# Moving the key, solution and delta-rule work of a woven decoder layer, and splitting its weight cuts over two steps

## The chip, the core and the metric

The kernel runs on one core of a Trainium2 chip. The core has a matrix engine (TensorE, PE in the profile), a vector engine (VectorE, DVE), a scalar engine (ScalarE, ACT), a general engine (GpSimd, POOL) and SyncE (SP), which here only issues transfers. Each engine works through its own list of instructions in order, and an instruction waits until the semaphores it names have been raised. Transfers (DMAs) are issued from the lists of SP, POOL and ACT. The metric is the device time in microseconds of one execution, as the median of several.

## The reference: what is computed

One inference step of a one-layer hybrid decoder over 512 new prompt tokens and 8 sampled tokens, all in float32, width 2048. Cut to what matters here:

```python
xn   = rmsnorm(h, norm_mix)
proj = xn @ w_in                      # columns: q | k | v | z | beta | decay | pool
qkv_c, new_conv = short_conv(conv_buf, qkv, conv_w)   # 4 taps, then silu
q = l2norm(q) * (DN_HEAD_DIM ** -0.5);  k = l2norm(k)
# gated delta rule, per head, chunks of the sequence:
a_mat = strict_lower(k k^T * beta * decay) + I
u, w  = triangular_solve(a_mat, v * beta), triangular_solve(a_mat, k * beta * exp(gc))
S     = S * exp(g_last) + k_dec^T @ (u - w @ S)       # from chunk to chunk
o     = (q * exp(g)) @ S + tril(q k^T * decay) @ v_new
dn_out   = rmsnorm(o, dn_norm) * silu(z)
pool_out = multiscale trailing-window mean minus token, times w_pool
h = h + concat(dn_out, pool_out) @ w_out
h = h + (silu(gate) * up) @ w_down    # gate, up = rmsnorm(h) @ w_gate_up
```

There are 8 heads of width 128. The matrix products must hold float32 accuracy. The kernel reaches it by cutting each operand into a high part `hi` and a low part `lo`, and adding three products: high by high, low by high and high by low.

## The kernel before, in words

**Stages.** On the profiled time axis: up to about 48 us the tokens are normalised and transposed; up to about 165 us the first column tiles of `w_in`, among them the eight tiles of keys, are multiplied in pairs, some of them by Strassen's scheme (`strassen`, with a callback `after(q, j)` that is called behind product j of pair q); from about 165 to 690 us runs the woven stage, which the change concerns; then follow the output projection, gate/up and down.

**The woven stage.** 28 column tiles of `w_in` and the pooling tiles are multiplied one after another, each with 96 matmuls (lines L184 to L186) in 16 steps of six. Between the steps a planner, class `Weave`, places side work: `weave.at(step, task)` starts a task, a Python generator, at a step, and each `yield n` in it says that its next piece comes n steps later. The planner runs when the program is built; what it fixes is the order of instructions on each engine. Tables at the top of the file give the starting steps: `KS` for the eight heads' `keys`, `ELIM` for the elimination, `D0` for the first delta rule. Nothing else than the order and the semaphores says when something runs.

**The tasks, in the order in which they come:**

- `keys(h)` loads the head's key columns, which the pair stage had stored to memory (`c_d`), and convolves them: one tap on ACT (L505), three on DVE (L508), silu on ACT (L510, with a load of its function table). The silu's result goes to PE: the Gram matrix of the keys (L1234) and transposes (L1237). ACT sums squares of the transposes (L1210), DVE forms the scales `sck`, the scaled Gram blocks `nn` (L1255) and scaled keys `kd` (L1257). `decay` (L1203) forms a decay mask `dm` from `gcb`, which is loaded from `gcr_d`. SP writes the diagonal 32x32 blocks of `nn` to `nd_d` and reads them back as `nb` (L1262, L1269), so that all heads' blocks lie side by side.
- `first_qv` loads and convolves q and v of head 0; `take_qv(h)` does it for the later heads, spread over the rule before.
- `eliminate` inverts all diagonal blocks at once, 31 pairs of DVE instructions (L1291, L1293), spread by an account of their work: a `yield` of one step for each 0.55 of `work`. SP writes the result to `ud_d` (L1303) and `load_u` reads it back as `utf`, for head 0 and then for head 1 (L1192, four transfers each).
- `delta(h)`, 26 steps for each head, solves with `utf` (matmuls from L1356 on, `uu` on DVE at L1377, matmul L1375) and runs the state from chunk to chunk: `R` (L1411), `W` on ACT (L1419), `S` (L1429) on DVE, with matmuls at L1408, L1416 and L1423 between them.
- sampled tokens' states (matmul L1511), and the pooling of the tiles, a run of DVE instructions from L1606 on.

**The weights' feed.** `feed` is called at every step. Every eight steps it loads half a tile of weights on SP (`feed_load`, 512 KB, L300) and cuts a half that was loaded 14 steps earlier (`feed_cut`, through `cut_raw`): `hi` on ACT (L308), then `lo` on DVE (L309), which reads `hi`. A product's tile goes from PE's accumulator to `ext` by DVE (L275), and POOL stores it to `c_d` (`stored`, L493).

Of the kernel before, what the change touches and what calls it, by code (L numbers as in the profile page):

```python
# [17 lines left out]
P = 128  # L18
# [8 lines left out]
FT = FF // P  # L27
EPS = 1e-6
POOLBUF = 15
KS, ELIM, D0 = (-5, 8, 21, 33, 44, 55, 66, 77), 104, 154  # L30
CHUNKS = ((0, 264), (264, 520))
HALF = NTOK // 2
FP = FT // 2
# [50 lines left out]
def decoder_kernel(ctx, tc, x_prompt, x_sample, state_delta, state_conv, state_pool, norm_mix, w_in,  # L84
# [410 lines left out]
    def convolution(x, t, place):  # L495

        ys = []

        def load():
            pool.memset(x[:, 0:3], 0.0)  # L500
            pool.dma_start(x[:, 3:3 + SEQ], c_d[t])

        def first():
            ys.append(place())
            act.activation(ys[0], x[:, 0:SEQ], AF.Copy, scale=cw(0, t))  # L505

        def tap(i):
            return lambda: dve.scalar_tensor_tensor(ys[0], x[:, i:i + SEQ], cw(i, t), ys[0], op0=ALU.mult, op1=ALU.add)  # L508

        return [load, first, tap(1), tap(2), tap(3), lambda: act.activation(x[:, 3:3 + SEQ], ys[0], AF.Silu)]  # L510

    def to_columns(o, t, ci, acc):
        c0, c1 = CHUNKS[ci]
# [288 lines left out]
    with tc.high_priority(offset=9 * AHEAD), tc.manual_schedule():  # L802
# [194 lines left out]
                b_raw[n] = load_raw(win_view(in_cols(b_order[n // 2]))[:, HG * (n % 2):HG * (n % 2) + HG, :])  # L997

        def feed_cut(n):
            if n in b_raw:  # L1000
                hi, lo = cut_raw(b_raw.pop(n))
                b_cut[n] = [(hi[:, k, :], lo[:, k, :]) for k in range(HG)]

        def feed(now):
            if (now + 10) % 8 == 0 and (now + 10) // 8 >= 2:
                feed_cut((now + 10) // 8)
            if now % 8 == 0:
                feed_load(now // 8 + 3)

# [4 lines left out]
        def after(q, j):  # L1014

            if (q, j) == (0, 1):
                gates(10)
            if q < len(pairs) - 1:
                return
            if j == 0:  # L1020
                pool.dma_start(b12, xs_d[0:8].rearrange("k p c -> p k c")[:, :, HALF:])
            if j == 2:
                nparts[1][0]()
            if j == 3:
                nparts[0][0]()
# [19 lines left out]
    with ExitStack() as p1:  # L1045
# [126 lines left out]
        def y_tile():  # L1172
            return d1tile("y", [P, SEQ], "y")

        def places(h):

            if h < 4:
                a, b = mixb[:, h, :], mixb[:, 4 + h, :]
            else:
                a, b = mixa[:, 4 + (h - 4) % 3, :], mixa[:, 7, :] if h % 2 == 0 else d1tile("vs", [P, SEQ], "nn")  # L1180
            return a[:, NB - 3:NTOK], b[:, 0:SEQ]

        def come_back(h):
            kd = kds[h] = d1tile("kd", [P, SEQ], "kd")
# [28 lines left out]


        def keys(h):
            x, nn = places(h)
            kT = x[:, 3:3 + SEQ]
            conv = convolution(x, 8 + h, y_tile)
            conv[0]()
            load_decay(h)  # L1220
            yield 5
            for f in conv[1:4]:
                f()
                yield 1
# [54 lines left out]
        def eliminate():  # L1279
# [7 lines left out]
            for t in range(31, 0, -1):  # L1287
                w = 32 - t
                tm = d1tile("tm", [P, 256], "tm")
                tv = tm[:, 0:t * w].rearrange("p (s j) -> p s j", j=w)  # L1290
                dve.tensor_tensor(tv, nb[:, 0:t, t:t + 1].broadcast_to([P, t, w]),  # L1291
                                  u[:, t:t + 1, t:32].broadcast_to([P, t, w]), op=ALU.mult)
                dve.tensor_tensor(u[:, 0:t, t:32], u[:, 0:t, t:32], tv, op=ALU.subtract)  # L1293
                work += 0.34 + t * w / 480
                if work > 0.55:
                    yield int(work / 0.55)
                    work %= 0.55
            ut = d1tile("nb", [P, 32, 32], "ut")
            dve.tensor_copy(ut, u.rearrange("p s j -> p j s"))
            utr = ut.rearrange("p s j -> p (s j)")  # L1300
# [15 lines left out]
        def take_qv(h):  # L1316
# [280 lines left out]
        def pooled(t, pe0, operands):  # L1597
# [74 lines left out]
        with tc.high_priority(offset=8 * AHEAD), tc.manual_schedule():  # L1672
            weave.feed = feed
            weave.add(states())
            for h in range(H):
                task = keys(h)
                if KS[h] < 0:
                    weave.at(KS[h] + next(task), task)
                else:
# [16 lines left out]
                    qkv_tile(t, w, 0 if i else 8)  # L1696
            pool_tiles((4, 5, 6), 20)
            w_last = weights_of(23)
            weave.feed = None
        p1.enter_context(tc.manual_schedule(engines={mybir.EngineType.PE}))  # L1700
        pool_tile(7, operands, w_last)
# [742 lines left out]
```

## Time and profile before

| What | Value |
|---|---|
| Median of 3 runs | 2235.96 us (2235.49 to 2237.29) |
| Profiled execution, its own time | 2237.41 us |
| Span of its profile | 2235.7 us |
| PE busy | 2153.5 us, 96% of the span |
| DVE, ACT, POOL busy | 79%, 43%, 21% |
| Mean granted clock of PE | 0.987 |

The profile shows one execution; times in it are microseconds from the start of its span. A row of the timeline gives start, duration, engine, line, operation, output <- inputs and shape, and in brackets how long the engine had been idle before it and what ended that. SPq is SP's list of transfers, where the duration is that of issuing. In a row that groups instructions stand the busy time and the mean of one in nanoseconds, then the idle time before them and its causes. A row of PE's waits gives the line, what it waited for, the total, the number of waits and the longest. "Granted clock" is the share of full clock that the chip let PE have.

### The profile page before, as it was taken

The page shows a single profiled execution, that of the slowest core. Times are in us where ns is not written, and L with a number is a line of the kernel's source. Part 1 is how long each engine was busy: PE and PEld are TensorE (multiplying, and loading weights), DVE is VectorE, ACT ScalarE, POOL GpSimd, SP SyncE. Part 2 cuts the span into 40 slices and gives each one's busy share as a digit, 9 for nine tenths or more (in the row PEclk, how much of TensorE's full clock was granted, in tenths as well). Part 3 has the DMA queues.
Part 4 walks back from the last instruction along what each step waited for, and adds up shares of the span by engine and source line. Part 5 has one row for each costly group of instructions (what it writes and reads, how often), then busy time and mean ns, then how long its engine had stood idle before and what let it go on. Part 6 is the DMA issues. An engine that isn't in the chain of part 4 may idle for free.

```text
span 2235.7 us, 43054 instructions
## 1 busy us (share of the span) xinstructions
PE 2153.5 (96%) x17737; PEld 2139.6 (96%) x17737; DVE 1771.9 (79%) x2612; ACT 970.4 (43%) x1476; POOL 480.2 (21%) x596
## 2 busy tenths in 40 slices
PE   7997888999999999999999999999999999999998
PEld 7997888998999999999999999999999999999998
DVE  7785674555649997989878888888888788887997
ACT  6344623444415555434434344343343534434554
POOL 2113321211101220233232332332102501103100
PEclk9999898999999999999999999999999999999999
DMA  8244543443243553455455454554444845537343
GB/s 266 76 133 135 148 145 103 131 120 88 73 137 117 163 154 96 138 154 151 141 166 148 141 156 145 165 147 137 138 133 133 281 128 163 158 108 229 98 114 115
DMA packets 449381, 316.99 MB, mean 142 GB/s; under 512 B 27808, under 2 KB 424505, under 8 KB 445841
## 3 DMA queue, kind: packets, MB, share of 16 engines
q1 hardware_dynamic: 424657, 223.14, 35.5%
q0 software_dynamic: 23360, 90.37, 12.4%
q8 instruction: 139, 2.28, 0.4%
q10 hardware_dynamic: 1168, 0.74, 0.1%
q14 instruction: 57, 0.47, 0.1%
HBM read 261.97 MB, written 52.87 MB: 141 GB/s over the span
## 4 chain that ended last, share of the span: by engine, by line
PE 67%; DVE 5%; ACT 2%; issue 1%; DMA 1%; POOL 0%; ACTq 0%; DVEq 0%; POOLq 0%
PE dn L316 20%; PE dn L315 20%; PE dn L317 20%; PE mm L184 1%; DVE lo L309 1%; PE mm L186 1%; PE mm L185 1%; DMA s<-in_state_delta_dram 1%; ACT hi L308 1%; DMA st<-a_d 1%; PE dn L1511 0%; DVE raw L337 0%; PE mm L315 0%; PE mm L316 0%; PE mm L317 0%
## 5 line engine op out<-in xcount | busy, mean ns | idle before, releaser
L309 DVE TENSOR_TENSOR lo<-raw,hi 128x1024 fp32r<-128x1024 f32 (+1 forms) x493 | 613.1, 1261 | 140.4 <-ACT hi L308 138.7
L308 ACT CAST hi<-raw 128x1024 fp32r<-128x1024 f32 (+1 forms) x493 | 501.2, 1029 | 464.0 <-DVE raw L337 218.1
L184 PE MATMUL mm<-xh,hi 128*128 128x264 f32 (+1 forms) x960 | 293.5, 306 | 5.2 <-DVE ext L275 3.8
L186 PE MATMUL mm<-xh,lo 128*128 128x264 f32 (+1 forms) x960 | 276.3, 288 | 2.8 <-DVE lo L151 2.1
L185 PE MATMUL mm<-xl,hi 128*128 128x264 f32 (+1 forms) x960 | 276.3, 288 | 1.3 <-DVE xl L620 1.1
L184 PEld LDWEIGHTS mm<-xh,hi 128*128 128x128 f32 x960 | 187.0, 195 | 6.0 <-DVE ext L275 4.0
L186 PEld LDWEIGHTS mm<-xh,lo 128*128 128x128 f32 x960 | 185.9, 194 | 3.7 <-DVE lo L151 2.7
L185 PEld LDWEIGHTS mm<-xl,hi 128*128 128x128 f32 x960 | 187.0, 195 | 1.9 <-DVE xl L620 1.9
L337 DVE TENSOR_TENSOR raw<-raw 128x1024 f32<-128x1024 f32 (+1 forms) x136 | 182.6, 1343 | 2.3
L316 PE MATMUL dn<-b21l,hi 128*128 128x260 f32 x620 | 175.7, 283 | 0.4 <-DVE b21l L2153 0.4
L317 PE MATMUL dn<-b21h,lo 128*128 128x260 f32 x620 | 175.4, 283 | 0.0
L315 PE MATMUL dn<-b21h,hi 128*128 128x260 f32 x620 | 174.9, 282 | 0.0
L317 PE MATMUL dn<-b11h,lo 128*128 128x260 f32 x612 | 173.2, 283 | 1.3 <-DVE lo L309 1.3
L316 PE MATMUL dn<-b11l,hi 128*128 128x260 f32 x612 | 173.3, 283 | 0.0
L315 PE MATMUL dn<-b11h,hi 128*128 128x260 f32 x612 | 172.7, 282 | 0.0
L315 PE MATMUL dn<-T1h,hi 128*128 128x260 f32 x556 | 158.1, 284 | 0.0
L316 PE MATMUL dn<-T1l,hi 128*128 128x260 f32 x556 | 157.7, 284 | 0.0
L1775 POOL TENSOR_TENSOR mixa<-mixa 128x520 f32<-128x520 f32 x22 | 51.4, 2334 | 494.5 <-DVE mixa L1769 494.5
L317 PE MATMUL dn<-T1h,lo 128*128 128x260 f32 x556 | 156.8, 282 | 0.0
L315 PE MATMUL dn<-B22h,hi 128*128 128x260 f32 x548 | 155.9, 284 | 0.0
L316 PE MATMUL dn<-B22l,hi 128*128 128x260 f32 x548 | 155.6, 284 | 0.0
L317 PE MATMUL dn<-B22h,lo 128*128 128x260 f32 x548 | 154.6, 282 | 0.4 <-DVE lo L309 0.4
(739 smaller groups left out, 6845.5 us busy)
## 6 DMA issues: line engine op xcount, KB each, us to landing
raw<-in_w_gate_up_dram SPq DMA_DIRECT2D x134, 512.0 KB
raw<-in_w_in_dram SPq DMA_DIRECT2D x75, 512.0 KB
a_d<-mixa POOLq DMA_DIRECT2D x22, 1040.0 KB, 5.5
raw<-in_w_down_dram SPq DMA_DIRECT2D x48, 448.0 KB
mixb<-in_w_gate_up_dram SPq DMA_DIRECT2D x41, 512.0 KB
raw<-in_w_out_dram SPq DMA_DIRECT2D x25, 512.0 KB
st<-a_d POOLq DMA_DIRECT2D x49, 260.0 KB, 6.5
raw<-in_w_down_dram SPq DMA_DIRECT2D x24, 512.0 KB
```

The lines of the kernel that those rows point to most:

```text
L184: te.matmul(acc[ci], wh, hi[k][:, c0:c1], start=(i == 0), stop=False)
L185: te.matmul(acc[ci], wh, lo[k][:, c0:c1], start=False, stop=False)
L186: te.matmul(acc[ci], wl, hi[k][:, c0:c1], start=False, stop=(i == len(w) - 1))
L308: act.copy(hi, raw)
L309: dve.tensor_tensor(lo, raw, hi.bitcast(F32), op=ALU.subtract)
L315: te.matmul(acc, wh[:, k, :], xf[:, k, :], start=start and k == 0, stop=False)
L316: te.matmul(acc, wh[:, k, :], xg[:, k, :], start=False, stop=False)
L317: te.matmul(acc, wl[:, k, :], xf[:, k, :], start=False, stop=stop and k == wh.shape[1] - 1)
L337: dve.tensor_tensor(r[name], r[a], r[b], op=op)
L1775: pool.tensor_tensor(q[:, 4:8:2, :], q[:, 1:4:2, :], q[:, 0:2, :], op=ALU.subtract)
```

## The change

It alters five things, all in the woven stage or just ahead of it.

1. **Keys.** `KS` becomes 4, 16, 28 ... 88, twelve steps apart, where it was -5, 8, 21, 33, 44, 55, 66, 77. A head's task no longer begins with its load and a pause of five steps, so that the Gram matmuls fall on steps 12, 24, 36, 48, 60, 72, 84, 96 (before: 9, 21, 34, 46, 57, 68, 79, 90). Heads 0 to 6 are loaded by SP during the last Strassen pair, head 7 at step 76. `place_k` says where a head's keys lie, `place_n` where its `nn` does.
2. **Loads of q and v** go from POOL's to SP's list too; 24 loads in all change list.
3. **Weights' feed.** `hi` is cut one step earlier than before (13 steps behind the load), `lo` where both stood before, a step later; a list `low_parts` carries it over.
4. **Elimination and delta rules.** `ELIM` goes from 104 to 111 and `D0` from 154 to 171; the elimination yields a step for each 0.48 of work.
5. **Pooling** writes its result `pw` into a part of `mixb` that is no longer used, instead of the buffer `y`.

```diff
-KS, ELIM, D0 = (-5, 8, 21, 33, 44, 55, 66, 77), 104, 154
+KS, ELIM, D0 = (4, 16, 28, 40, 52, 64, 76, 88), 111, 171
...
-        def load():
+        def load(eng=pool):
             pool.memset(x[:, 0:3], 0.0)
-            pool.dma_start(x[:, 3:3 + SEQ], c_d[t])
+            eng.dma_start(x[:, 3:3 + SEQ], c_d[t])
...
         def feed_cut(n):
-            if n in b_raw:
-                hi, lo = cut_raw(b_raw.pop(n))
-                b_cut[n] = [(hi[:, k, :], lo[:, k, :]) for k in range(HG)]
+
+            hi, lo = [wpl.tile([P, HG * P], F32R, tag=x, name=x) for x in ("hi", "lo")]
+            raw = b_raw.pop(n)
+            b_cut[n] = [tuple(x[:, P * k:P * k + P] for x in (hi, lo)) for k in range(HG)]
+            act.copy(hi, raw)
+            return lambda: dve.tensor_tensor(lo, raw, hi.bitcast(F32), op=ALU.subtract)
+
+        low_parts = []
 
         def feed(now):
-            if (now + 10) % 8 == 0 and (now + 10) // 8 >= 2:
-                feed_cut((now + 10) // 8)
+            if low_parts:
+                low_parts.pop()()
+            n = (now + 11) // 8
+            if (now + 11) % 8 == 0 and n in b_raw:
+                low_parts.append(feed_cut(n))
             if now % 8 == 0:
                 feed_load(now // 8 + 3)
...
+            if (q, j) == (2, 1):
+                for h in range(2, 7):
+                    convolution(place_k(h), 8 + h, None)[0](sp)
+            if (q, j) == (2, 4):
+                for h in range(2):
+                    convolution(place_k(h), 8 + h, None)[0](sp)
...
-            conv[0]()
             load_decay(h)
-            yield 5
+            if h == 6:
+                convolution(place_k(7), 15, None)[0](sp)
...
-                if work > 0.55:
-                    yield int(work / 0.55)
-                    work %= 0.55
+                if work > 0.48:
+                    yield int(work / 0.48)
+                    work %= 0.48
...
-                v[0]()
+                v[0](sp)
...
-            return [q[0], load_v, lambda: None, lambda: None, *q[1:5], lambda: (q[5](), v[1]()), *[lambda i=i: v[i]() for i in range(2, 6)]]
+            return [lambda: q[0](sp), load_v, lambda: None, lambda: None, *q[1:5], lambda: (q[5](), v[1]()), *[lambda i=i: v[i]() for i in range(2, 6)]]
...
-            pw = d1tile("y", [P, NTOK], "pw")
+            pw = mixb[:, t % 2, :]
...
-                if KS[h] < 0:
-                    weave.at(KS[h] + next(task), task)
-                else:
-                    weave.at(KS[h], task)
+                weave.at(KS[h], task)
```

Lines below the edits move: L308 and L309 of the feed become L1008 and L1009, the lines of `keys`, `decay`, `load_u` and `delta` grow by 13 (L1234 is L1247, L1356 is L1369).

**The loads of the keys.** POOL's list before, from the last store of the pair stage to the stage's first steps (`nt` are rows of the incoming states):

```order
L493 DMA c_d<-ext 128x512
L1021 DMA mixb<-xs_d 128x8x260
L500 MEMSET mixb 128x3
L501 DMA mixb<-c_d 128x512
L1088 DMA nt<-in_state_conv_dram 128x4x128
L1083 DMA nt<-in_state_conv_dram 64x128
L1088 DMA nt<-in_state_pool_dram 128x4x128
L1088 DMA nt<-in_state_pool_dram 128x3x128
L1083 DMA nt<-in_state_pool_dram 64x128
L500 MEMSET mixb 128x3
L501 DMA mixb<-c_d 128x512
L1147 MEMSET utf_2066 128x1024
```

and SP's list after the change, over the same stretch:

```order
L300 DMA raw<-in_w_in_dram 128x8x128 x3
L501 DMA mixb<-c_d 128x512 x2
L501 DMA mixa<-c_d 128x512 x3
L145 DMA raw<-in_w_in_dram 128x8x128 x2
L501 DMA mixb<-c_d 128x512 x2
L300 DMA raw<-in_w_in_dram 128x8x128 x2
L1209 DMA gcb<-gcr_d 128x512
```

Head 1's load stood on POOL behind the five transfers of states; now seven heads' loads stand on SP around the last weights of the stage before (L145).

**The solution's way to head 0.** SP's list before, behind the elimination:

```order
L1303 DMA ud_d<-u 28x4x1024
L1303 DMA ud_d<-ut 28x4x1024
L300 DMA raw<-in_w_in_dram 128x8x128
L1196 DMA gcb<-gcr_d 128x512
L1192 DMA utf_2066<-ud_d 32x8x32 x4
L1192 DMA utf_2068<-ud_d 32x8x32 x4
L300 DMA raw<-in_w_in_dram 128x8x128 x3
```

and after the change:

```order
L1316 DMA ud_d<-u 28x4x1024
L1316 DMA ud_d<-ut 28x4x1024
L300 DMA raw<-in_w_in_dram 128x8x128
L1205 DMA utf_2080<-ud_d 32x8x32 x4
L1209 DMA gcb<-gcr_d 128x512
L1205 DMA utf_2082<-ud_d 32x8x32 x4
L300 DMA raw<-in_w_in_dram 128x8x128
L501 DMA qT<-c_d 128x512
```

The decay vector `gcb` of head 0 came ahead of head 0's `utf`; now it stands between head 0's and head 1's. Head 1's q (`qT`) is new in this list.

**The cuts in a delta rule.** ACT's list before, at the start of head 1's rule:

```order
L1350 ACT_TABLE_LOAD
L1350 ACTIVATE gcb<-gcb 128x512
L1358 COPY xt__4182<-dn 128x384
L1359 ACTIVATE dm<-dm 128x512
L1210 ACTIVATE junk,ss<-dn 128x128 x4
L1210 ACTIVATE junk,so<-dn 128x128 x4
L308 CAST hi<-raw 128x1024
L505 ACTIVATE y<-qT,prm 128x512
```

and after the change:

```order
L1008 CAST hi<-raw 128x1024
L1363 ACT_TABLE_LOAD
L1363 ACTIVATE gcb<-gcb 128x512
L1371 COPY xt__4307<-dn 128x384
L1372 ACTIVATE dm<-dm 128x512
L1223 ACTIVATE junk,ss<-dn 128x128 x4
L1223 ACTIVATE junk,so<-dn 128x128 x4
L505 ACTIVATE y<-qT,prm 128x512
```

The cast `hi` moved from behind the eight sums of squares to ahead of the rule's first work on ACT. DVE's `lo` still stands just ahead of the rule's first `uu` there.

More of the change, by code (lines that the diff above doesn't have):

```diff
@@ L510, in convolution, with place_k @@
         return [load, first, tap(1), tap(2), tap(3), lambda: act.activation(x[:, 3:3 + SEQ], ys[0], AF.Silu)]
+    def place_k(h):
+        return (mixb[:, h, :] if h < 4 else mixa[:, 4 + (h - 4) % 3, :])[:, NB - 3:NTOK]
     def to_columns(o, t, ci, acc):
@@ L1173, in y_tile, with place_n @@
             return d1tile("y", [P, SEQ], "y")
-        def places(h):
-            if h < 4:
-                a, b = mixb[:, h, :], mixb[:, 4 + h, :]
-            else:
-                a, b = mixa[:, 4 + (h - 4) % 3, :], mixa[:, 7, :] if h % 2 == 0 else d1tile("vs", [P, SEQ], "nn")
-            return a[:, NB - 3:NTOK], b[:, 0:SEQ]
+        def place_n(h):
+            return (mixb[:, 4 + h, :] if h < 4 else d1tile("vs", [P, SEQ], "nn") if h % 2 else mixa[:, 7, :])[:, 0:SEQ]
         def come_back(h):
@@ L1215, in keys @@
         def keys(h):
-            x, nn = places(h)
+            x, nn = place_k(h), place_n(h)
             kT = x[:, 3:3 + SEQ]
             conv = convolution(x, 8 + h, y_tile)
-            conv[0]()
             load_decay(h)
-            yield 5
+            if h == 6:
+                convolution(place_k(7), 15, None)[0](sp)
             for f in conv[1:4]:
@@ L1676, in decoder_kernel @@
                 task = keys(h)
-                if KS[h] < 0:
-                    weave.at(KS[h] + next(task), task)
-                else:
-                    weave.at(KS[h], task)
+                weave.at(KS[h], task)
             weave.at(ELIM - 12, first_qv())
@@ L1698, in decoder_kernel @@
             w_last = weights_of(23)
+            assert not low_parts
             weave.feed = None
```

## The prediction

> **What bounds the kernel now.** I read the page first: which engine is full.
>
> ```profile
> PE 2153.5 (96%) x17737; PEld 2139.6 (96%) x17737; DVE 1771.9 (79%) x2612; ACT 970.4 (43%) x1476; POOL 480.2 (21%) x596
> ```
>
> TensorE (PE) is busy 96% of the span, so the kernel is bound by its matmuls, and only what delays PE can be won. Next I cut the span into stretches; after the stretch come its length, then busy us and instructions of PE, PE's weight loads, DVE, ACT and POOL, then the granted clock.
>
> ```profile
> 165.00:290.00 125.00, 100.44 (x768) 98.14 (x768) 76.38 (x194) 65.29 (x130) 45.20 (x103) 0.92 0.52 148
> 290.00:345.00 55.00, 39.73 (x296) 39.09 (x295) 35.49 (x84) 12.29 (x19) 5.99 (x12) 0.83 0.46 126
> 345.00:605.00 260.00, 241.23 (x1999) 237.35 (x1998) 150.38 (x343) 108.48 (x259) 39.94 (x80) 0.96 0.36 103
> 860.00:2000.00 1140.00, 1138.39 (x9451) 1137.69 (x9450) 976.33 (x1157) 477.33 (x621) 288.34 (x257) 1.00 0.51 149
> ```
>
> From 860 on there is nothing to win. The loss sits in the woven stage: PE idles 24.6 us during the keys (165 to 290), 15.3 during the elimination (290 to 345) and 18.8 during the delta rules (345 to 605), 58.6 in all. A weave step is six matmuls; at 1138.39/9451 = 0.12 us each that is 0.72 us. Then the waits of PE (total, times, longest):
>
> ```profile
> PE dn L1234 <- ACT mixb L510: 16.8, 3, 9.3
> PE dn L1356 <- DMA utf<-ud_d: 10.8, 1, 10.8
> PE dn L1375 <- DVE uu L1377: 7.3, 4, 3.0
> PE dn L1234 <- ACT mixa L510: 4.6, 3, 3.0
> PE mm L184 <- DVE ext L275: 3.8, 1, 3.8
> PE dn L1408 <- DVE S L1429: 3.1, 3, 1.3
> ```
>
> The keys' Gram matmul (L1234) waits 21.4 us for the silu, the first delta rule (L1356) 10.8 for the solution, the later rules mostly for DVE. Stalls also cost clock:
>
> ```profile
> 195.00:200.00 5.00, 5.00 (x25) 5.00 (x25) 2.48 (x4) 4.61 (x12) 1.49 (x7) 0.52 0.21 52
> 380.00:385.00 5.00, 4.71 (x31) 4.71 (x32) 2.83 (x12) 0.00 (x0) 2.65 (x4) 0.66 0.14 42
> ```
>
> After a long stall PE works at about half clock (25 matmuls in 5 us where 41 would fit). Over the three stretches the missing clock is 0.08 x 125 + 0.17 x 55 + 0.04 x 260 = 29.8 us; what falls into the idle time itself costs nothing, and I put the paid part at 7, 5 and 8, 20 us. So about 78 us are at stake.
>
> The second row follows a stall of only 1.9 us (shown below). The Trainium skill (TensorE: Matmul & The Clock Gate, "What's actually happening") has the clock halve after an idle window of about 3.4 us. By that rule the delta rules' short stalls would cost no clock; the row says they do, so the trace disagrees, and I keep the 8 us.
>
> **Keys.** POOL's, ACT's and PE's timelines at the two worst heads:
>
> ```profile
> 177.42 0.59 POOL L501 DMA_DIRECT2D mixb<-c_d  x1
> 184.87 0.72 ACT L505 ACTIVATE y<-mixb,prm 128x512 f32<-128x512 f32 x1 [5.05 <-DMA mixb<-c_d]
> 194.61 2.08 PE L1234 MATMUL dn<-mixb 128*128 128x128 f32 x8 [6.53 <-ACT mixb L510]
> 221.88 0.72 ACT L505 ACTIVATE y<-mixb,prm 128x512 f32<-128x512 f32 x1 [6.52 <-DMA mixb<-c_d]
> 228.86 1.01 PE L1234 MATMUL dn<-mixb 128*128 128x128 f32 x3 [9.30 <-ACT mixb L510]
> ```
>
> Heads 1 and 3 start their convolution 5.05 and 6.52 us late. For head 1 POOL issued the load at 177.42, 7.5 us before the tap, behind five other transfers. The change issues these loads before the stage, which takes 6.53 to 1.5 and 9.30 to 2.8. What remains is a loop: a head's convolution is queued behind the sums of squares that need the previous head's PE products. Its parts:
>
> ```profile
> L1210 ACT ACTIVATE junk<-dn 128x128 f32<-128x128 f32 x35 | 9.7, 276 | 3.2 <-PE dn L1237 2.1
> L1210 ACT ACTIVATION_READ_ACCUMULATOR junk<-dn 128x1 f32 x35 | 6.8, 194 | 0.0
> L505 ACT ACTIVATE y<-mixb,prm 128x512 f32<-128x512 f32 x4 | 2.9, 724 | 13.4 <-DMA mixb<-c_d 11.6 <-DVE mixa L536 1.7
> L510 ACT ACT_TABLE_LOAD x8 | 10.3, 1283 | 31.9 <-DVE y L508 31.9
> L510 ACT ACTIVATE mixb<-y 128x512 f32<-128x512 f32 x4 | 2.5, 630 | 1.3 <-issue 1.3
> L508 DVE SCALAR_TENSOR_TENSOR y<-mixb,prm,y 128x512 f32<-128x512 f32 x12 | 9.3, 772 | 6.4 <-ACT y L505 6.4
> L1255 DVE SCALAR_TENSOR_TENSOR mixb<-dn,sck,dm 128x128 f32<-128x128 f32 x16 | 4.8, 340 | 0.0
> L1257 DVE TENSOR_TENSOR kd<-dn,sck 128x512 f32<-128x512 f32 x8 | 5.4, 677 | 0.0
> L309 DVE TENSOR_TENSOR lo<-raw,hi 128x1024 fp32r<-128x1024 f32 x19 | 23.2, 1219 | 15.5 <-ACT hi L308 15.5
> ```
>
> About 1.2 us of matmuls, 4 x (0.28 + 0.19) of squares, 0.72, three taps 2.3, four `nn` 1.4, `kd` 0.7, silu with its table load 1.9: some 10 us, 1.2 more where a `lo` falls in. PE needs 12 steps, 8.6 us, plus 1.4 for the eight small matmuls: 10.0. The two are level, so a wait stays wherever `lo` or an eviction joins. By heads: 1.5 and 2.8 as above; head 2 (the third mixb wait, 16.8 - 6.53 - 9.30 = 1.0) loses a step (0.7): 1.7; heads 4 to 7 gain a step each, which takes their three waits, 4.6 together, to 2.9. That is 8.9. For heads 4 to 7 the third tap now comes behind all of `nn` and `kd` (at most 2 x 0.34 + 0.68 = 1.36 more each, 5.4); against that `lo` no longer makes DVE wait for `hi` (15.5 us in this stretch). I take 10.5. Idle falls by 11, the paid clock from 7 to 4: **14 us saved**, bounds 6 (the longer tap order counts in full and the clock stays) and 22 (the loop never binds).
>
> **Elimination.** The 3.8 us of L184 is a tile whose accumulator waits for an eviction behind the elimination on DVE, which comes behind head 0's q and v taps:
>
> ```profile
> L505 ACT ACTIVATE y<-qT,prm 128x512 f32<-128x512 f32 x1 | 0.7, 726 | 5.0 <-DMA qT<-c_d 5.0
> ```
>
> So it starts 5 us late for want of one load. That load moves to SP, 12 steps ahead as before, where no POOL work stands in front; and the elimination is spread over 21.9/0.48 = 45.6 steps instead of 21.9/0.55 = 39.8 (its work by the code's own sum), so evictions get more gaps: 3.8 to about 0.5, with 1.7 of clock: **5 us saved**, bounds 0 and 6.5.
>
> **The solution's way to head 0.** SP's queue, with what DVE and PE waited for:
>
> ```profile
> 323.92 0.68 SPq L1303 DMA_DIRECT2D ud_d<-u  x1
> 327.49 2.57 SPq L300 DMA_DIRECT2D raw<-in_w_in_dram  x1
> 330.12 2.56 SPq L1196 DMA_DIRECT2D gcb<-gcr_d  x1
> 332.79 7.66 SPq L1192 DMA_DIRECT2D utf<-ud_d  x8
> 340.15 1.14 DVE L1203 SCALAR_TENSOR_TENSOR dm<-gcb,gcs,mneg 128x128 f32<-128x128 f32 x4 [13.69 <-DMA gcb<-gcr_d]
> 340.88 0.93 PE L1356 MATMUL dn<-utf,mixb 128*128 128x96 f32 x3 [10.75 <-DMA utf<-ud_d]
> ```
>
> From the first write to PE's start are 17.0 us. The rule now starts 171 - 156.6 = 14.4 steps after the elimination's end by plan, instead of 154 - 143.8 = 10.2: 4.2 steps, 3.0 us more cover. `gcb` (2.56 us of issuing) goes behind head 0's four `utf` loads: 10.75 - 3.0 - 2.6 = 5.1. But then `gcb` lands last, and `dm` (1.14), ACT's exponentials and the copy of PE's product queue behind it; at worst all 2.6 come back. I take 6, with the paid clock from 3 to 2: **5.5 us saved**, bounds 1 and 9.
>
> **Delta rules.** One stall in full, on DVE and PE:
>
> ```profile
> L309 DVE TENSOR_TENSOR lo<-raw,hi 128x1024 fp32r<-128x1024 f32 x27 | 33.0, 1223 | 24.1 <-ACT hi L308 24.0
> 378.55 1.22 DVE L309 TENSOR_TENSOR lo<-raw,hi 128x1024 fp32r<-128x1024 f32 x1 [4.29 <-ACT hi L308]
> 380.29 0.38 PE L1375 MATMUL dn<-uu,xt__4182 128*96 128x64 f32 x2 [1.90 <-DVE uu L1377]
> 585.93 0.69 DVE L1606 TENSOR_TENSOR pes<-pe 128x518 f32<-128x518 f32 x1
> 590.70 0.35 DVE L1429 SCALAR_TENSOR_TENSOR S<-S,egl,dn 128x128 f32<-128x128 f32 x1
> ```
>
> DVE had 4.29 us with nothing to do, since `lo` waits for `hi` and `hi` stood behind eight sums of squares on ACT; `uu`, and PE with it, came after. With `hi` a step earlier and, at head 1, ahead of the squares, and `lo` between the rules' own operations, most of the 7.3 and 3.1 goes: 10 of 18.8 us idle, with `lo` itself (1.22) hidden in the time DVE waits for PE. Two things speak against: ACT's copy `xt` now stands behind a `hi` (about 1 us, where PE is late anyway), and the rules run 17 steps later, so that three instead of two pooling bursts (585.93 to 590.70, 4.8 us of DVE) meet heads 6 and 7: I add 2.5, at most 4.8. Idle 18.8 to 11.3, clock 8 to 5: **10.5 us saved**, bounds 3 and 21.
>
> **Costed at nothing or little.** 24 loads go from POOL to SP, whose queue is idle between weight loads; the five ahead of the stage's first weights are for tiles stored long before. If those weights were held up, the stage would start up to 3 us late. Tasks behind the rules come 10 steps later; PE work is the same. I add 2 us, 0 to 5. Memory conflicts: none counted.
>
> **Sum.** 14 + 5 + 5.5 + 10.5 - 2 = 33. The profiled execution took 2237.4 us (span 2235.7), so 2204.4 in its terms; it lies 1.4 above the median of 2235.96, and I forecast **2203 us**. All bounds at once would give 5 to 58.5 saved; the terms are nearly independent, so the forecast's own range is 2192 to 2215.
>
> **Rivals.** *The keys' loop still binds and DVE's stalls only move*: 6 + 2 + 4 + 6 - 1 = 17 saved, **2219**. For it: loop and PE are level at 10 us; against it: 11.6 us of the first tap's wait hung on loads alone. *SP becomes the queue that holds up the weights*: a q load stands in SP's order ahead of a weight load; if each of the eight heads' loads waits for its store and holds the weights by more than 33/8 = 4.1 us, `hi` and then L184 stall, at half clock, and the time goes above 2236, I say **2245**. For it: `gcb` and weight each took 2.6 us to issue; against it: weights are issued 13 steps, 9.4 us, before `hi`, and ACT's casts waited for no weight in the rules:
>
> ```profile
> L308 ACT CAST hi<-raw 128x1024 fp32r<-128x1024 f32 x27 | 28.1, 1041 | 0.0
> ```
>
> The Trainium skill (DMA: Bandwidth & Descriptors, "Issuing engines are not separate DMA queues") says that loads from all issuing engines share the same 16 DMA engines, so that moving them brings only the issuing time; no row here measures that, and my terms rest on issuing earlier. *No change*: one late step (the solution, say) gives back what the others win, **2236**. *The skill's clock rule after all*: the 3 us of clock in the delta rules are not won, **2206**.
>
> **Chances.** Forecast 0.66, loop 0.20, SP 0.06, no change 0.05, clock rule 0.03. A measurement tells 0.2%, 4.5 us. Faster: 0.66 + 0.20 + 0.03, less 0.02 for a slip beyond the cases: 0.87; same 0.06; slower 0.07. To leave out no more than 2 in 10 the range takes in the loop's case: 2190 to 2224.
>
> **What would show it.** In the changed kernel: no wait of ACT's first tap for `c_d` and L1234's successor idle 8 to 13 us; the solution's wait 4 to 8 us, with `gcb` landing after `utf`; DVE's `lo` waiting for `hi` under 5 us where it was 39.6; clock at least 0.95 in the keys. I am wrong if waits on the silu stay near 20 us, if ACT's `hi` waits for weights, or if the rules idle 18 us again.

## The result, and the profile after

The changed kernel takes 2219.1 us (median of 6 executions, 2213.18 to 2224.86) where the kernel before takes 2235.72 (6 executions, 2231.83 to 2237.29): a ratio of 0.9927, 95% interval 0.9909 to 0.9945, 16.6 us saved. The forecast was 2203. The direction was right, the size was not: half of the expected gain is missing. The time lies outside the forecast's own range (2192 to 2215), and inside the wider one (2190 to 2224), which had been drawn to take in a rival. The profiled execution took 2216.79 us, 20.6 less than that of before.

The first row is of the page, the others are the same kind of stretches as before, cut at the new boundaries (keys to 275, elimination to 327, rules to 590, then the rest of the woven stage; columns as in the prediction):

```profile
PE 2148.4 (97%) x17737; PEld 2135.9 (96%) x17737; DVE 1773.2 (80%) x2612; ACT 970.2 (44%) x1476; POOL 469.5 (21%) x572
```

```profile
165.00:275.00 110.00, 95.66 (x728) 93.00 (x727) 72.91 (x188) 64.04 (x128) 37.59 (x80) 0.94 0.53 152
275.00:327.00 52.00, 50.58 (x422) 50.37 (x421) 39.09 (x90) 11.46 (x12) 9.37 (x21) 1.00 0.50 147
327.00:590.00 263.00, 243.33 (x2052) 240.68 (x2052) 161.20 (x369) 118.14 (x278) 34.24 (x68) 0.97 0.38 108
590.00:680.00 90.00, 79.76 (x646) 78.74 (x646) 51.72 (x111) 28.66 (x46) 1.60 (x6) 0.94 0.37 103
```

The keys' and the elimination's stretches have improved: PE idles 14.3 and 1.4 us where it idled 24.6 and 15.3. The rules idle 19.7 us as before (18.8), and behind them, where the kernel before lost 2.6 us in 95 (605 to 700), PE now idles 10.2 in 90. PE's waits say at whom:

```profile
PE dn L1421 <- DVE S L1442: 7.2, 3, 3.8
PE mm L1729 <- ACT xh L210: 6.7, 1, 6.7
PE dn L1247 <- ACT mixb L510: 5.8, 3, 3.2
PE dn L1247 <- ACT mixa L510: 5.5, 4, 2.4
...
PE dn L1478 <- DVE mixb L1472: 3.3, 2, 3.1
...
PE dn L1421 <- DVE S L1440: 3.1, 1, 3.1
PE dn L1524 <- DMA s<-in_state_delta_dram: 3.0, 2, 1.8
PE dn L1388 <- ACT xt__6454 L1371: 2.3, 1, 2.3
...
PE dn L1388 <- ACT xt__5726 L1371: 1.9, 1, 1.9
...
PE dn L1369 <- DMA utf<-ud_d: 1.5, 1, 1.5
```

The keys wait 5.8 + 5.5 = 11.3 us (21.4 before), the solution 1.5 (10.8), the eviction of the elimination not at all (3.8). The first two rows are where new waits have come: PE waited for S 3.1 and 0.4 us before (L1429, L1427) and now 7.2 and 3.1 (L1442, L1440), and the output projection (L1729) waits 6.7 us for a split on ACT that had made PE wait 0.2.

**By parts.** I summed PE's waits of over 0.3 us in the timelines of all kernels, by the part of the woven stage in which they end. "Rules" are those between the first rule's start and some nine steps behind the last one's end, "tail" what comes then up to the output projection's first products (710 us). "Idle in all" is what PE's busy time leaves of the stretch from 160 to 710; besides the parts it holds some 3 us at the stage's entry, the same in all, and the waits under 0.3 us. The clock that was paid is the missing clock times PE's busy time in stretches of 5 us, from 160 to 710.

| Kernel | keys | elimination | solution | rules | tail | idle in all | clock paid |
|---|---|---|---|---|---|---|---|
| before | 21.2 | 4.5 | 10.8 | 18.5 | 2.2 | 61.1 | 18.7 |
| changed | 11.4 | 0 | 1.5 | 19.1 | 11.4 | 46.9 | 14.0 |
| before, cuts split | 20.3 | 4.5 | 10.3 | 11.8 | 3.3 | 54.0 | 12.0 |
| changed, cuts not split | 13.5 | 2.1 | 2.0 | 19.4 | 9.6 | 50.1 | 18.5 |
| changed, D0 161 | 10.2 | 0 | 9.5 | 13.7 | 4.3 | 41.1 | 12.5 |
| changed, hi three steps ahead | 10.9 | 0 | 1.7 | 11.7 | 10.7 | 38.4 | 11.8 |

Changed against before: 14.2 us idle and 4.7 us clock, 18.9 of the 20.6 us between the two profiled executions. The question for the experiments is the columns of the rules and the tail. A row is one execution, and its clock is partly chance, as the last section shows.

**A stall in the rules.** ACT, DVE and PE at the largest one, in head 2:

```profile
400.13 1.28 ACT L510 ACT_TABLE_LOAD   x1
401.42 0.63 ACT L510 ACTIVATE qT<-y 128x512 f32<-128x512 f32 x1
402.13 0.72 ACT L505 ACTIVATE y<-vT,prm 128x512 f32<-128x512 f32 x1
402.76 0.41 ACT L1583 ACTIVATE mixa<-mixa 128x264 f32<-128x264 f32 x1
403.07 1.03 ACT L1008 CAST hi<-raw 128x1024 fp32r<-128x1024 f32 x1
404.13 1.23 DVE L1009 TENSOR_TENSOR lo<-raw,hi 128x1024 fp32r<-128x1024 f32 x1 [3.49 <-ACT hi L1008]
405.28 0.34 DVE L1442 SCALAR_TENSOR_TENSOR S<-S,egl,dn 128x128 f32<-128x128 f32 x1
405.67 0.58 PE L1421 MATMUL dn<-S,mixb 128*128 128x128 f32 x1 [3.76 <-DVE S L1442]
```

It is the mechanism of before at another place. There eight sums of squares stood ahead of `hi`; here the next head's silu, its table load, a tap and an activation of a product's tile (L1583) do, 2.9 us from 400.13 to `hi`. One step, 0.72 us, is not enough lead. The same at 532.50 in head 6 costs 2.7 us. A second kind is the pooling run:

```profile
518.84 0.70 DVE L1619 TENSOR_TENSOR pes<-pe 128x518 f32<-128x518 f32 x1
...
522.91 0.70 DVE L211 TENSOR_TENSOR dl<-mixb,dh 128x520 fp32r<-128x520 f32 x1 [0.69 <-ACT dh L210]
523.53 0.28 DVE L1440 COPY S<-dn 128x128 f32<-128x128 f32 x1
523.87 0.58 PE L1421 MATMUL dn<-S,mixb 128*128 128x128 f32 x1 [3.11 <-DVE S L1440]
```

4.8 us of DVE in one piece, and S behind it (head 6). Two more such runs end at the copy `xt` of head 7 (2.3 us) and at the gate of head 7 (L1478, 3.1 us).

**The tail.** DVE, ACT and PE at the end of the stage:

```profile
657.52 0.28 DVE L1554 SCALAR_TENSOR_TENSOR mixa<-sc_qts,prm,mixa 128x64 f32<-128x64 f32 x1
...
660.20 2.21 ACT L210 CAST xh<-mixa 128x520 fp32r<-128x520 f32 x4 [1.94 <-DVE mixa L219]
660.88 0.59 PE L1729 MATMUL mm<-xh,hi 128*128 128x260 f32 x1 [6.75 <-ACT xh L210]
```

L1554 is the last operation of the sampled tokens' chain. Their tasks begin only when the last rule has ended (at step 379 by plan instead of 369), so the chain ends, at 657.8, after PE has run out of tiles, at 654.1, and the output projection, which begins with `mixa`, waits.

### The profile page after: what moved, and what is told of

Same layout as the page of the kernel before. It is cut to its first block, busy times and chain, and to the rows that moved or that the text cites. A ratio compares the mean times of both kernels' runs of the same rounds, so it can differ in the third digit from the quotient of the medians.

```text
span 2215.1 us, 43081 instructions
## 1 busy us (share of the span) xinstructions
PE 2148.4 (97%) x17737; PEld 2135.9 (96%) x17737; DVE 1773.2 (80%) x2612; ACT 970.2 (44%) x1476; POOL 469.5 (21%) x572
## 3 DMA queue, kind: packets, MB, share of 16 engines
q0 software_dynamic: 21440, 84.07, 11.6%
## 4 chain that ended last, share of the span: by engine, by line
PE 67%; DVE 5%; DMA 2%; ACT 1%; issue 1%; POOL 0%; ACTq 0%; DVEq 0%; SPq 0%; POOLq 0%
PE dn L316 20%; PE dn L315 20%; PE dn L317 20%; PE mm L184 1%; DVE lo L309 1%; PE mm L185 1%; PE mm L186 1%; DMA st<-a_d 1%; DMA s<-in_state_delta_dram 0%; DVE raw L337 0%; PE dn L1524 0%; ACT hi L308 0%; PE mm L315 0%; PE mm L316 0%; PE mm L317 0%
## 5 line engine op out<-in xcount | busy, mean ns | idle before, releaser
L308 ACT CAST hi<-raw 128x1024 fp32r<-128x1024 f32 (+1 forms) x447 | 453.3, 1028 | 445.5 <-DVE raw L337 217.3
L309 DVE TENSOR_TENSOR lo<-raw,hi 128x1024 fp32r<-128x1024 f32 (+1 forms) x447 | 556.8, 1265 | 102.7 <-ACT hi L308 101.2
L184 PE MATMUL mm<-xh,hi 128*128 128x264 f32 (+1 forms) x960 | 291.8, 304 | 1.5 <-ACT hi L149 1.5
L184 PEld LDWEIGHTS mm<-xh,hi 128*128 128x128 f32 x960 | 185.9, 194 | 2.0 <-ACT hi L149 1.9
```

The lines of the kernel that those rows point to most:

```text
L184: te.matmul(acc[ci], wh, hi[k][:, c0:c1], start=(i == 0), stop=False)
L308: act.copy(hi, raw)
L309: dve.tensor_tensor(lo, raw, hi.bitcast(F32), op=ALU.subtract)
```

## The experiments

Theory, from the trace: the split of the cuts works, but the new start of the rules (D0 171) takes its gain back, by pooling runs that meet the rules and by the sampled states' late chain. Rivals: the split does nothing, since ACT is blocked ahead of `hi` anyway; it is the phase of the rules against the eight-step cuts, not their lateness; the queue from which the loads are issued matters. Each kernel is given with its median, the kernel before's median on the same chip, and the ratio.

### The split alone, and everything but the split

The changed kernel with both cuts at one step:

```diff
-            n = (now + 11) // 8
-            if (now + 11) % 8 == 0 and n in b_raw:
-                low_parts.append(feed_cut(n))
+            n = (now + 10) // 8
+            if (now + 10) % 8 == 0 and n in b_raw:
+                feed_cut(n)()
```

> The changed kernel with the weights' cuts as before: hi and lo at the same step, lo right behind. If the split over two steps is what shortened DVE's wait for hi (39.5 us in the stage before, 21.1 changed), the wait goes back above 35 us and the time rises by 5 to 12 us over the changed kernel's 2219, to 2224 to 2231. Rival: the order of the keys and the earlier loads did it and hi is held up by what stands before it on ACT, not by its step: within 4 us of 2219.

Measured: 2223.1 against 2236.48, 0.9942 (0.9927 to 0.9957): 13.4 us saved. DVE's wait for `hi` went back as expected (below), but the time rose by 4 us only, under the 5 to 12. And the kernel before with nothing but the split of the feed:

> The kernel before, with only the cuts split over two steps. If the split is worth what I put on the rules (10.5 us forecast), 2224 to 2230, with DVE's wait for hi falling from 39.5 us to 20 or less and the rules' waits on uu and S (10.4 us) to half. Rival: ACT is blocked ahead of hi as often, the waits only change place: 2233 to 2238.

Measured: 2222.13 against 2236.48, 0.9936 (0.9922 to 0.9951): 14.3 us saved, a little more than expected, with a wait of 22.9 us where I had put 20 or less. DVE's waits for `hi` in the woven stage, in the kernel before, before with the split, changed, and changed without the split:

```profile
DVE lo L309 <- ACT hi L308: 39.5, 21, 4.6
```

```profile
DVE lo L1004 <- ACT hi L1003: 22.9, 15, 3.5
```

```profile
DVE lo L1009 <- ACT hi L1008: 21.1, 11, 5.3
```

```profile
DVE lo L1009 <- ACT hi L1008: 43.7, 21, 5.7
```

The split halves the wait in both settings. In the kernel before that is worth 14.3 us: 6.7 us less idle in the rules (18.5 to 11.8) and 6.7 us less clock (18.7 to 12.0). In the changed kernel it is worth some 4 us, with intervals that overlap (0.9927 to 0.9957, 0.9909 to 0.9945); by the table it helps there the keys and the elimination (13.5 to 11.4, 2.1 to 0) and the clock (18.5 to 14.0), and leaves the rules where they were (19.4 to 19.1). The two halves of the change save 13.4 and 14.3 us alone and 16.6 together. So the rival that the split does nothing falls, and part of the missing gain is an interaction in the rules: what the split wins there at the old start, it does not win at the new one. The tail's cost is another part, and it stands without the split too (9.6 us).

### The rules' start

Ten steps earlier:

```diff
-KS, ELIM, D0 = (4, 16, 28, 40, 52, 64, 76, 88), 111, 171
+KS, ELIM, D0 = (4, 16, 28, 40, 52, 64, 76, 88), 111, 161
```

> The changed kernel with D0 161 in place of 171. If the rules' lateness cost the tail, the 6.7 us wait of the output projection and the 3.0 us of the sampled states' matmuls go (with some 2 us of clock, 11 us won), while the first rule's wait for the solution grows from 1.5 by ten steps, 7.2 us, to 8.7 (with 2 us of clock, 9 lost): 2213 to 2221. Rival: the tail's wait comes from the pooling result's place in mixb or from the weights and stays at 6 us: then 2225 to 2230.

Measured: 2207.66 against 2236.48, 0.9874 (0.9858 to 0.9891): 28.8 us saved, 12 more than the change and better than either expectation. PE's waits:

```profile
PE dn L1369 <- DMA utf<-ud_d: 9.5, 1, 9.5
PE dn L1421 <- DVE S L1442: 6.9, 3, 3.8
```

L1729 has gone from the list and L1524 fell from 3.0 to 1.1: the tail's cost is the rules' lateness (the sampled tokens' tasks begin at step 369 again, as in the kernel before). The solution's wait grew by 8.0 us for ten steps, as expected. What I had not expected is the rules' own part, 19.1 to 13.7. By the timelines the larger share is the cuts: S behind `lo` costs one wait of 2.4 us (at 436) instead of 3.8 and 2.7. The pooling runs still meet S twice, for 3.8 and 2.6 us (at 534 and 557), 6.4 us instead of 8.5. A start later by ten steps thus bought 8 us at the solution for 7 in the tail, 5.5 in the rules, and clock.

One step earlier, which puts the eight-step cuts on the same places of the rules as in the kernel before (154 and 170 leave the same remainder):

> The changed kernel with D0 170 in place of 171, so that the cuts, which come every eight steps, fall on the same places of the rules as with 154. If this phase is what cost the rules their gain, PE's idle time in the rules falls from 19.5 to 11 to 14 us and the time to 2208 to 2213. Rival: the lateness alone counts: the solution's wait grows by 0.7, the tail's falls by 0.7, and the time stays at 2217 to 2221.

Measured: 2215.01 against 2234.34, 0.9912 (0.9896 to 0.9929). Between the two expectations, but idle in the rules went only to 16.2, far from the 11.8 of the same phase at the old start: the phase alone does not explain it. The rules' longest waits are at other operations than at D0 171:

```profile
PE dn L1429 <- DVE R L1424: 6.5, 3, 3.6
...
PE dn L1388 <- DVE uu L1390: 4.7, 3, 3.1
```

With the elimination at 0.55 per step again, and D0 165:

> The changed kernel with the elimination spread at 0.55 of work per step as before (39.8 instead of 45.6 steps) and D0 165, so that the solution's way has the same cover and the rules and the tail come 6 steps earlier. If the tail's cost goes by the rules' start, the output projection's wait falls from 6.7 to about 2.5 and the time to 2209 to 2216. Rival: the faster elimination brings the accumulators' wait back (3.8 us before) and the total stays at 2217 to 2222.

Measured: 2212.55 against 2236.48, 0.9896 (0.9881 to 0.991). The tail's idle fell from 11.4 to 4.3 us; the accumulators' wait came back with 0.8 us only. The solution's wait, which I took to stay the same, was 5.1: DVE does not keep the pace of 0.55 per step, so the elimination did not end 5.8 steps earlier as its plan says. SP's first write behind it stands at 314.98 us, against 314.68 in the changed kernel.

### What stands ahead of `hi`

`hi` three steps ahead of `lo` instead of one, `lo` where it was:

```diff
-            if low_parts:
+            if low_parts and (now + 10) % 8 == 0:
                 low_parts.pop()()
-            n = (now + 11) // 8
-            if (now + 11) % 8 == 0 and n in b_raw:
+            n = (now + 13) // 8
+            if (now + 13) % 8 == 0 and n in b_raw:
```

> The changed kernel with hi cut three steps ahead of lo instead of one. If the remaining stalls of S behind lo come from hi standing behind a head's silu and its table load on ACT, DVE's wait for hi falls from 21.1 us to under 10, the waits on S at L1442 from 7.2 to under 2 and the time to 2209 to 2214. Rival: hi then stands ahead of xt and the squares elsewhere or its weights are not there yet, and waits on xt or for the weights take the place: 2217 to 2223.

Measured: 2205.33 against 2234.34, 0.9868 (0.9853 to 0.9883): 29.0 us saved. DVE's wait for `hi`:

```profile
DVE lo L1009 <- ACT hi L1008: 8.3, 4, 3.5
```

21.1 to 8.3; the waits on S at L1442 left PE's list (the 3.76 us above and 2.7 us in head 6) but for 0.75 us, the rules' idle fell to 11.7, and the time by more than I gave it. At the place of the stall shown above, ACT now runs the cast while it would have been idle, ahead of the copy `W` and the silu with its table load (399.75):

```profile
395.59 1.05 ACT L1008 CAST hi<-raw 128x1024 fp32r<-128x1024 f32 x1 [0.77 <-PE mm L185]
```

In the kernel before the same edit, on top of the split:

> The kernel before with the cuts split, hi three steps ahead of lo in place of one (2222 with one). If hi standing behind other work on ACT is what is left of DVE's wait for it (22.9 us), it falls under 10 us and the time to 2212 to 2219. Rival: with the old start of the rules the split had already won what there is: 2220 to 2224.

Measured: 2213.58 against 2235.65, 0.9901 (0.9886 to 0.9915), 22.1 us saved by the cuts alone. DVE's wait for `hi` is 3.0 us there and the rules' idle 7.5. At the same cuts, then, the rules idle 7.5 us with the old start and 11.7 with the new one; this 4 us is about what the new start costs in the rules when `lo` hardly waits. The three pooling collisions (3.1, 2.3 and 3.1) are the longest waits at the new start, and the only ones over 0.3 us left there behind 510 us, 8.5 us; at the old start the rules' waits behind 510 us come to 2.4 us (1.2, 0.5 and 0.7).

### The pooling runs

Tiles 4, 5 and 6 pooled three steps after the tile's end (with the tile's buffer taken when its first half is evicted):

```diff
-            for _ in pooled(t, pe0, operands):
-                if weave.now <= SPLIT:
-                    pass
+            late = pooled(t, pe0, operands)
+            if t in (4, 5, 6):
+                weave.at(weave.now + 3, late)
+            else:
+                next(late)
```

> The changed kernel with the pooling run of tiles 4, 5 and 6 three steps later than the end of the tile. If the pooling runs are what stands before S, the copy xt and the gate at heads 6 and 7 (3.1, 2.3 and 3.1 us), these three waits fall to 3 us in all and the time to 2211 to 2215. Rival: the run then stands before another operation of the same rules, and the time stays at 2216 to 2222.

Measured: 2220.65 against 2234.34, 0.994 (0.9925 to 0.9955), no gain over the change. The waits moved instead of going:

```profile
PE dn L1478 <- DVE mixb L1472: 3.4, 2, 3.1
...
PE dn L1436 <- ACT W L1432: 2.5, 1, 2.5
PE mm L184 <- ACT hi L1008: 2.1, 1, 2.1
```

The S copy of head 6 and `xt` of head 7 no longer wait, but PE waits 2.5 us for W and 2.1 for a later `hi`, and S behind `lo` in head 6 costs 3.5 us instead of 2.7; the gate's wait did not move at all, since tile 7 was left as it was. The operations of a rule's chain are two or three steps (1.4 to 2.2 us) apart, a run is 4.8 us long. That is why I take it that no step suits the whole run; only this one was tried, so it is argued, not shown.

### The queue of the loads

> The changed kernel with the 24 loads of keys, q and v issued from POOL's list again, at the same places. If issuing early is what counts, the keys' waits stay at 11.3 us and the time within 4 us of the changed kernel's 2219. If the queue itself matters (POOL's transfers standing behind its other work), head 0's q comes late again, the accumulator's wait of 3.8 us and some of the keys' waits return, and the time rises by 4 to 10 us.

Measured: 2221.94 against 2234.34, 0.9947 (0.993 to 0.9964); the interval overlaps the change's. The keys wait 7.2 + 4.4 = 11.6 us instead of 11.3, L184 waits for no eviction, and the solution's wait is 3.1 us instead of 1.5. What the loads gained, they gained by being issued early; the list they are in made no difference that this measures, which agrees with the Trainium skill (DMA: Bandwidth & Descriptors, "Issuing engines are not separate DMA queues").

### Together

> Hi three steps ahead of lo (2205 by itself) and D0 161 (2208 by itself, 11 us under the changed kernel) together. If the two act on different stalls (S behind lo there, the tail here), 2193 to 2199: no wait of the output projection on ACT, the solution's wait near 9 us, DVE's wait for hi under 10 us. Rival: D0 161 gained in the rules by its phase, which hi's earlier step has already won: 2201 to 2206.

Measured: 2203.72 against 2235.65, 0.9858 (0.9844 to 0.9873), 31.9 us saved: the rival was right, the two gains overlap. D0 161 takes 9.5 us at the solution, and the rules idle 10.1 us where `hi` alone leaves 11.7.

> Hi three steps ahead of lo and D0 165. The tail's wait falls from 6.7 to about 2.5, the solution's grows from 1.7 to about 6: if only these two trade, 2204 to 2208, no better than D0 171; if the phase of the rules against the pooling runs decides, as D0 161 suggests, 2196 to 2203.

Measured: 2205.99 against 2235.65, 0.9866 (0.985 to 0.9883): a trade of solution (7.3 us) and tail (4.2), nothing won. The last kernel takes `hi` three steps ahead at D0 171 and shortens the sampled states instead:

```diff
-                    if j != 1:
+                    if j != 1 and (hf, j) != (1, 0):
                         yield 1
```

> Hi three steps ahead of lo with the rules' start as in the change (D0 171; 2205 by itself), and the sampled tokens' state products spread over five steps a head instead of six, so that they end eight steps, 5.8 us, earlier. If the tail's 6.7 us wait is the sampled states' chain ending late, it falls to 1 to 2 us and the time, with the clock that goes with it, to 2197 to 2200. Rival: the chain is bound by the loads of the states, each of which then has less time: the matmuls wait for them (2.3 us before) by 5 us or more, and the time stays at 2203 to 2207.

Measured: 2204.09 against 2235.18, 0.9857 (0.984 to 0.9874), four executions from 2199.32 to 2205.73. The wait of 6.7 us is gone, so it was the sampled states' chain; in its place PE waits 2.9 us for splits and 2.7 for the states' loads (2.3 without the edit, where the rival had 5 or more). Idle in all is the lowest of all kernels, 35.1 us. But the time is the rival's, and the profiled execution was only 1.3 us shorter than without the edit (2204.14 to 2205.45): 3.3 us less idle, 1.7 us more clock paid (13.5 against 11.8). Where such clock goes can be seen at a wait that both have in the same place, with the same length; PE's timeline and the stretch from there, first without the edit, then with it:

```profile
576.36 0.44 PE L1478 MATMUL dn<-ident,mixb 128*128 128x128 f32 x2 [3.06 <-DVE mixb L1472]
```

```profile
576.00:581.00 5.00, 4.64 (x39) 4.64 (x40) 3.38 (x7) 1.96 (x3) 0.00 (x0) 1.00 0.00 0
```

```profile
576.30 0.47 PE L1478 MATMUL dn<-ident,mixb 128*128 128x128 f32 x1 [3.06 <-DVE mixb L1472]
```

```profile
576.00:581.00 5.00, 4.70 (x21) 4.70 (x22) 2.00 (x5) 1.59 (x2) 0.00 (x0) 0.50 0.01 3
```

The kernel without the edit keeps full clock behind a stall of 3.06 us, the one with it works at half clock: 39 against 21 matmuls. That one stall's clock is decided otherwise in two executions, whose programs differ only in what comes behind it. They ran on two chips; but the kernel with the loads on POOL's list, which ran on the same chip as the one without the edit, also lost the clock behind the same stall of 3.06 us (0.50 and 21 matmuls from 588 to 593).

## Why the prediction was right or wrong

**What bounds the kernel**: right. PE is the bound, the stage is the woven one, 61 us idle from 160 to 710 and 18.7 us of clock (I had 58.6 in three stretches, and 20).

**Keys**, 14 us forecast: right about the waits, not about the clock. The waits on silu are 11.3 us, forecast 10.5, and the loads' part is as read from the rows: ACT's first taps no longer wait for `c_d`,

```profile
L505 ACT ACTIVATE y<-mixb,prm 128x512 f32<-128x512 f32 x4 | 2.9, 716 | 1.7 <-DVE mixa L540 1.7
```

and the waits of 6.53 and 9.30 became 1.84 (head 1, forecast 1.5) and 0.83 (head 3, forecast 2.8); head 2 has 3.17 (forecast 1.7) and heads 4 to 7 have 5.5 together (forecast 2.9, and 1.6 more in what I took). That the sum came out is partly luck: head 3's error makes up for the others'. The paid clock in the keys, which I had falling from 7 to 4, fell from 6.7 to 5.9. The rival that the loop binds gave 2219, which is the time measured, but by a mechanism that did not happen.

**Elimination**, 5 us: right, no wait on an eviction is left (4.5 us by the table).

**The solution's way**, 5.5 us: too careful, 1.5 us of wait remain where I had 6. SP's list after, with DVE and PE:

```profile
314.68 0.68 SPq L1316 DMA_DIRECT2D ud_d<-u  x1
318.25 1.08 SPq L300 DMA_DIRECT2D raw<-in_w_in_dram  x1
319.44 3.66 SPq L1205 DMA_DIRECT2D utf<-ud_d  x4
323.14 0.45 SPq L1209 DMA_DIRECT2D gcb<-gcr_d  x1
327.66 1.14 DVE L1216 SCALAR_TENSOR_TENSOR dm<-gcb,gcs,mneg 128x128 f32<-128x128 f32 x4 [8.86 <-DMA gcb<-gcr_d]
327.06 1.10 PE L1369 MATMUL dn<-utf,mixb 128*128 128x96 f32 x8 [1.48 <-DMA utf<-ud_d]
```

The way from the first write to PE's start shrank by 4.6 us (17.0 to 12.4), not by the 2.6 of `gcb` alone: the weights' load took 1.08 us to issue instead of 2.57, which no term foresaw. The cover grew by 4.7 us (from 6.2 to 10.9 between the first write and PE's arrival), not 3.0. `gcb` did land after `utf`, by 0.6 us, and cost nothing, where I had kept up to 2.6 for it.

**Delta rules**, 10.5 us: this is the step that failed. The gain itself ("most of the 7.3 and 3.1 goes") held at the old start, where the split alone took 6.7 us of idle out of the rules (18.5 to 11.8) and 14.3 us off the time; the term added that gain to rules at a new start as if nothing else stood there. The rules idle 19.1 us, forecast 11.3. I had looked only at what stood ahead of `hi` where the trace of before had its stalls, not at what stands there at the new steps, a silu with its table load: 3.76 and 2.7 us, and DVE's `lo` still waits 21.1 us for `hi` where the forecast had under 5. With `hi` three steps ahead both stalls go. "I add 2.5, at most 4.8" for the pooling runs: their three waits are 3.1 + 2.3 + 3.1 = 8.5 us, read from the timelines. "ACT's copy `xt` now stands behind a `hi` (about 1 us, where PE is late anyway)": PE waits 1.9 us for it in head 5, and 0.9 with `hi` three steps ahead, so the price was right, but PE was not late.

**Costed at little**, 2 us, 0 to 5: the second failed step. "Tasks behind the rules come 10 steps later; PE work is the same" overlooked that these tasks feed the output projection. The slack stood in the trace of before, in the end of the chain on DVE and the projection's first matmul, which began without a wait:

```profile
676.93 0.28 DVE L1541 SCALAR_TENSOR_TENSOR mixa<-sc_qts,prm,mixa 128x64 f32<-128x64 f32 x1
684.29 0.28 PE L1718 MATMUL mm<-xh,hi 128*128 128x260 f32 x1
```

The chain ended at 677.2, 7.1 us ahead of the projection. The splits between them take 3.1 us where the projection waits for them (657.8 to 660.88 in the changed kernel), which leaves some 4 us of slack, and ten steps are 7.2. The chain now ends 3.7 us behind PE's last tile instead of 7.1 ahead of it. Idle in the tail grew by 9.2 us, with 2.7 of clock. The five loads ahead of the weights cost nothing, as said.

**Sum.** The terms of the forecast, and what they came to: idle by the table of parts, clock by the stretches of 5 us of each part.

| Term | forecast, us saved | measured idle + clock |
|---|---|---|
| Keys | 14 | 9.8 + 0.8 = 10.6 |
| Elimination and solution | 5 + 5.5 = 10.5 | 13.8 + 4.0 = 17.8 |
| Delta rules | 10.5 | -0.6 + 2.8 = 2.2 |
| Tasks behind the rules | -2 | -9.2 - 2.7 = -11.9 |
| Sum | 33 | 18.7 |

The profiled executions differ by 20.6 us. The two failed steps, together 8.5 us in the forecast, lost 9.7; that the error was no larger is owed to the solution, which won more than I gave it. Of the signs named beforehand, the one against me came: the rules idle 18 us again.

**Rivals.** SP did not hold up weights, and no wait of ACT's `hi` on weights shows in the changed kernel. On the clock: PE lost it behind stalls far below 3.4 us also here (195 to 200, behind 1.84 us: 0.66), so the trace goes on disagreeing with the Trainium skill's idle window of about 3.4 us (TensorE: Matmul & The Clock Gate, "What's actually happening"), but not behind each such stall.

```profile
405.00:410.00 5.00, 4.33 (x20) 4.33 (x21) 3.28 (x7) 0.42 (x1) 0.00 (x0) 0.50 0.54 131
585.00:590.00 5.00, 3.41 (x29) 3.41 (x29) 3.58 (x8) 2.22 (x3) 1.16 (x4) 1.00 0.12 33
195.00:200.00 5.00, 5.00 (x32) 5.00 (x31) 2.30 (x11) 4.25 (x12) 1.13 (x2) 0.66 0.32 94
```

These are stretches of the changed kernel behind waits of 3.76, 3.06 and 1.84 us; the second kept full clock.

What stays open: how the 8.5 us of the pooling runs could be had (cutting the run into pieces was not tried), and how large the cost of the rules' new start is apart from the chance of the clock, since each part was read from one execution.

## What to carry to other kernels

Moving a task later in a hand-planned order is paid at the far end: look up the slack of the last consumer of everything behind it before counting the wait that goes at the near end. A stall seen in a trace tells what is late at the old steps; at the new steps the same operation stands behind other work, so each queue has to be read again there. Where a producer and its consumer stand on two engines, as `hi` and `lo` do, one step of lead may leave the producer behind the same long work; it needs enough to stand ahead of it. Here that work was 2.9 us of ACT's, and three steps put `hi` in front of it, where one did not.

## What the runs showed of the hardware

A stall of the same 3.06 us at the same place cost half clock for the next 5 us in one execution (0.50) and nothing in another (1.00). In the changed kernel 1.84 us was enough at 194 and 3.06 not at 586. So in these runs the price of a stall of 1.8 to 3.8 us was its length, or up to some 3 us more, and nothing that differs ahead of it in the trace says which. (Behind the 3.76 us it was 0.5 x 4.33 = 2.2 us in the row at 405 above, and 0.2 and 0.4 in the rows beside it.) That may be why the changed kernel's six executions spread over 11.7 us and the kernel before's over 5.5: the slowest of the six has a mean clock of 0.986, the fastest of 0.991, and 0.005 of 2215 us is an estimated 11 us. That link is argued, not shown.

The time that SP needs to issue a transfer of one size was not the same: 512 KB of weights took 2.57 us before and 1.08 after at the same place of the program, behind the elimination's writes, and the 256 KB of `gcb` 2.56 and 0.45, where the change had moved it by four small loads. Within the changed kernel alone one `gcb` took from 0.34 to 2.80 us. What decides it, no run here shows.
